# Feature rows of a bidirectional RWKV-7 scan by one transpose per head and chunk, the gate's low-rank job ahead of the second key job, feature loads held back

## Chip, core and metric

One NeuronCore of a Trainium2 chip runs the whole kernel in one launch. The time is the device time of an execution in microseconds, smaller is better; the figure for a kernel is the median of its runs. All data are float32 in HBM. TensorE (PE) takes them as fp32 matmuls, or as fp32r matmuls on operands split into a high and a low part.

## The reference: what is computed

One layer of a diffusion backbone on 128 context tokens and 1024 latent tokens of width 1024, here laid side by side as T = 1152 columns:

```
h = rmsnorm(x, norm1_g) * (1 + sc1) + sh1
r, k, v, wdf, wdb, adf, adb, gd, cb, cc, cx, gates = split(h @ w_in)
# per direction d (forward, backward), per head of 64:
decay = exp(-exp(w_log(tanh(wd) @ w2)));  a = sigmoid(a0 + ad @ a2);  k_d = k * (1 + (a - 1) * k_a)
sa = S @ (-kk);  S = S * decay + sa (x) (kk * a) + v (x) k_d;  y = S @ r      # step by step in t
o_a = (group_norm(y_f + y_b) + bonus) * (sigmoid(gd) @ gate_g2)
o_b = cb * conv3(cc * cx)
x = x + gt1 * ((g_a * (o_a @ w_pa) + g_b * (o_b @ w_pb)) @ w_o)
x = x + gt2 * (conv_ffn(rmsnorm(x, norm2_g) ...) @ w_down)
```

Outputs are both token streams after a final rmsnorm, and the context's final states S of both directions. The scan is computed in chunks of 64 tokens: inside a chunk b (kk * a) and k_d, each scaled by decays, meet the features of kk and r in 64x64 products, and the triangular system of a chunk is solved by repeated products.

## The kernel before

**Dense work.** `build` makes a list `jobs`; a job is one 128-row tile of `w_in` or of another weight. Each weight tile is loaded (`wraw`), split into `whi` and `wlo` on ACT, DVE or POOL, and multiplied with the activations `h` in three thirds (`th`) of 384 columns: 24 matmuls of 128x384 per third, 72 per job, into one of three PSUM banks `psd`. After each third its evacuation runs (`k_evac`, `r_evac`, `gd_evac` and so on). The order of the list is written out by hand at L685 to 692: low-rank jobs WD and AD, then `rkv(0)` (K0, R0, V0), `rkv(1)`, the gate's low-rank job `T_GD`, the 24 fp32 matmuls of `gjobs` (the gate's second weight g2, loaded as in_g2, on the three `gz` of `gd_evac`), then for each of eight m `rkv(m+2)` and branch b, and the two gates.

**Buffers.** `gz` of `gd_evac` (L560) and `kt` of `k_evac` (L614), and two tiles of branch b, share a pool tag `rot` with four buffers. A kt is squared (`ksq`), reduced per head on PE (`kps`), brought to a reciprocal root on ACT (`kr`), and last read by kr<-kt,par,kr on DVE; `gz` is last read by the matmuls psd<-gz,wraw. `st` has four buffers too.

**The scan.** `Scan` runs beside the dense jobs as a set of streams. `drive` steps a stream between two dense matmuls when a condition holds and its time on a model clock (`K.clk`) has come; a priority scheduler then orders each engine's instructions. A pair p is two heads on 128 partitions, and pp is two pairs. `prep_all` (L1022) computes the features of a pair and a third (`prep`) from the low-rank products (`lps` out of `llo`), kk and r, and writes them to DRAM as FA (kk and r) and FB (b and k), one DMA for each per segment, with all 128 partitions. 36 items (4 pp x 9 chunk pairs, 8 blocks e each) go through `prep2_all` (L1040): wait for `ready`, load `E`, `O` (FA by head parity) and `BK` (FB), then `prep2`: the gram matmuls `gpb` and `gpk` (64x64 weights from BK, 64x128), the scaling of BK by the decay on ACT, and the transposition of BK to token rows (`bps`, evacuated to `BT`). bps is 32 fp32 matmuls per item against a 64x64 identity, one for each e, head h and a (b or k), into the half `HS[h if a else 1 - h]` of PSUM. Then `chain` (31 doubling steps on DVE), `merge` (mps), `scan` (px and py, the state `Wt`) and `finish` (fps). A scan step is px<-SX,G, DVE's copy of the state (Wt, L1387), px<-Wt,BT and py<-G,Wt.

**Queues.** Nearly all DMAs are issued by SP, in order; an issue that has to wait for a buffer or for data holds up all behind it. fb<-ak in the profile is the write of FB, BK<-fb, E<-fa and O<-fa the loads of an item, gs<-gz the write of the gate's result.

Of the kernel before, what the change touches and what calls it, by code (L numbers as in the profile page):

```python
# [22 lines left out]
C = 64  # L23
# [9 lines left out]
T_R, T_K, T_V, T_WD, T_AD, T_GD, T_CB, T_CC, T_CX, T_GA, T_GB = 0, 8, 16, 24, 25, 26, 27, 35, 43, 51, 59  # L33
# [308 lines left out]
def build(tc, ins, outs, dbg=None):  # L342
    K = Kern(tc, ins, outs)
# [3 lines left out]
    with es:  # L347
# [162 lines left out]
        with ExitStack() as ea:  # L510
# [130 lines left out]
            def rkv(m):  # L641
                job(T_K + m, k_evac(m))
                job(T_R + m, r_evac(m))
                job(T_V + m, v_evac(m))
# [38 lines left out]
                return ev  # L683

            rkv(0)  # L685
            rkv(1)
            job(T_GD, gd_evac)
            gjobs()
            for m in range(8):
                if m + 2 < 8:  # L690
# [293 lines left out]
class Scan:  # L984
# [4 lines left out]
    def __init__(self, K, const, apool, par, pc, mask, ident, bones, x0, hw0, hka, oka, dr):  # L989
        self.K, self.nc, self.pc, self.dr = K, K.nc, pc, dr  # L990
        self.mask, self.ident, self.bones, self.x0 = mask, ident, bones, x0
        self.hw0, self.hka, self.oka = hw0, hka, oka
        self.eps = const.tile([P, 1], F32, name="gneps", tag="gneps")
        K.nc.gpsimd.memset(self.eps, GN_EPS)
        self.psx = apool("psx", 1, PSUM)
        self.psy = apool("psy", 1, PSUM)
        self.psm = apool("psm", 3, PSUM)
        self.sets = apool("sets", 3)
        self.one = apool("one", 1)
        self.two = apool("two", 2)  # L1000
        self.ys = apool("ys", 4)
        self.fin = apool("fin", 1)
        self.drp = apool("drp", 2, DRAM)
        nc = K.nc
        self.reset = self.one.tile([P, TH], F32, name="reset", tag="reset")
        nc.gpsimd.memset(self.reset, 1.0)
        nc.gpsimd.memset(self.reset.rearrange("p (c t) -> p c t", t=C)[:, :, 0:1], 0.0)
        self.e65 = self.one.tile([P, 6, C + 1], F32, name="e65", tag="e65")
        nc.gpsimd.memset(self.e65[:, :, 0:1], 1.0)
        self.lwl = self.one.tile([P, 4, P], F32R, name="lwlo", tag="lwlo")  # L1010
        nc.gpsimd.memset(self.lwl[64:128].bitcast(F32), 0.0)
        self.items = [(pp, n) for pp in range(4) for n in range(9)]
        self.info = {}

        self.W = self.one.tile([P, 2, 4, 2, C], F32, name="Wt", tag="Wt")
        self.y, self.PC = {}, {}
        self.NY = 4

    def start(self):
        K = self.K  # L1020
        ev = K.events
        N = len(self.items)  # L1022

        def prep_all(s):
            yield lambda: ("kk", 0, 0) in ev and ("r", 0, 0) in ev
            self.lora_in(0, 0)
            for p in range(NPAIR):
                yield lambda: ("kk", p, 0) in ev and ("r", p, 0) in ev
                yield from self.lora_w(s, p)
                for th in (0, 2, 1):  # L1030
                    yield lambda: ("kk", p, th) in ev and ("r", p, th) in ev
                    yield from self.prep(s, p, th)
                    ev.add(("prep", p, th))

        def ready(i, what):
            pp, n = self.items[i]
            ths = {n // 3, (7 - n) // 3} if n < 8 else {2}
            return all((what, 2 * pp + q, th) in ev for q in range(2) for th in ths)

        def prep2_all(s):  # L1040
            for i, (pp, n) in enumerate(self.items):
                yield lambda: ready(i, "prep") and (i < 3 or ("scan", i - 3) in ev)
                self.features(s, i, pp, n)
                s.t = K.clk.now + 2500
                yield
                yield from self.prep2(s, i, pp, n)
                ev.add(("prep2", i))

        def vfill_all(s):
            for i, (pp, n) in enumerate(self.items):  # L1050
                yield lambda: ready(i, "v")
                yield from self.vfill(s, i, pp, n)

        def load_all(s):
            for i in range(N):
                yield lambda: ("gram", i) in ev and (i < 2 or ("chain", i - 2) in ev)
                self.chain_load(i)
                s.t = K.clk.now + 2000
                yield
                ev.add(("load", i))  # L1060

        def chain_all(s):
            for i in range(N):
                yield lambda: ("load", i) in ev
                yield from self.chain(s, i)
                ev.add(("chain", i))

        def merge_all(s):
            for i in range(N):
                yield lambda: ("chain", i) in ev  # L1070
                s.t = K.clk.now + 5000
                yield
                yield from self.merge(s, i)
                ev.add(("merge", i))

        def scan_all(s):
            for i, (pp, n) in enumerate(self.items):
                yield lambda: ("merge", i) in ev and ("prep2", i) in ev
                yield from self.scan(s, i, pp, n)
                ev.add(("scan", i))  # L1080
                if n >= 4:
                    key = 7 - n if n < 8 else 8
                    K.spawn(lambda s2, pp=pp, key=key: self.finish(s2, pp, key), 4, gate=1000, ahead=0)

        K.spawn(scan_all, 0, ahead=0)
        K.spawn(merge_all, 0.5, ahead=0)
        K.spawn(vfill_all, 0.7, ahead=600)
        K.spawn(chain_all, 2, ahead=100)
        K.spawn(load_all, 1.5, ahead=0)
        K.spawn(prep2_all, 1, ahead=-300)  # L1090
        K.spawn(prep_all, 3, gate=1500, ahead=1000)
# [14 lines left out]
    def prep(self, s, p, th):  # L1106
# [15 lines left out]
        for d in range(2):  # L1122
# [52 lines left out]
            for a, b in segs:  # L1175
                g0 = t0 + a if d == 0 or t0 + a >= TL else TL - t0 - b
                K.act(s, PC[:, q, d, g0 // C:(g0 + b - a) // C], e65[:, a // C:b // C, C], AF.Copy)
                for dst, src in (("FA", FAo), ("FB", B)):
                    K.dma(dr[dst][pp][:, q, d, 2 * g0:2 * (g0 + b - a)],
                          src[:, a // C:b // C].rearrange("p c a t -> p (c a t)"), "fa")  # L1180
            yield

    def lora_in(self, th, d):
# [24 lines left out]
    def prep2(self, s, i, pp, n):  # L1208
        K = self.K
        E, O, G, BT, BK = (self.info[i][k] for k in ("E", "O", "G", "BT", "BK"))  # L1210


        HS = [slice(0, 64), slice(64, 128)]
        for q in range(2):
            es = slice(4 * q, 4 * q + 4)
            gb, gk = [self.psm.tile([P, 512], F32, name=nm, tag="psm").rearrange("p (c t) -> p c t", t=2 * C)
                      for nm in ("gpb", "gpk")]
            calls = []
            for e in range(4 * q, 4 * q + 4):
                for ps, a in ((gb, 1), (gk, 0)):  # L1220
                    for h in range(2):
                        o = HS[h if a else 1 - h]
                        calls.append(lambda ps=ps, a=a, h=h, e=e, o=o: K.mm(
                            ps[o, e - 4 * q, :], BK[HS[h], e, a, :], (E, O)[h][HS[h], e, :], True, True, 85))
            K.group(calls)
            s.t = K.clk.now
            mk = lambda sl: self.mask[sl].to_broadcast([sl.stop - sl.start, 4, 2 * C])
            K.tt(s, G[:, es, :], gb, mk(slice(0, P)), ALU.mult)
            for h in range(2):
                o = HS[1 - h]  # L1230
                K.tt(s, (E, O)[h][o, es, :], gk[o], mk(o), ALU.mult)
            yield
        self.to_blocks(s, i)
        K.events.add(("gram", i))
        yield
        yield lambda: i < 2 or ("scan", i - 2) in K.events

        for x in range(4):
            for c in range(2):
                b = BK[:, 2 * x + c].rearrange("p a t -> p (a t)")  # L1240
                K.act(s, b, b, AF.Identity, scale=self.PCc(i, c)[:, x])
        yield
        pv = [self.psm.tile([P, 512], F32, name="bps", tag="psm").rearrange("p (e t) -> p e t", t=C) for _ in range(2)]
        K.group([lambda e=e, a=a, h=h: K.mm(pv[h][HS[h if a else 1 - h], e, :], BK[HS[h], e, a, :],
                                            self.ident[HS[h], HS[h]], True, True, 45)
                 for e in range(8)[::-1] for a in range(2) for h in range(2)])
        s.t = K.clk.now
        for h in range(2):
            K.act(s, BT[:, h], pv[h], AF.Copy)
        yield  # L1250
# [282 lines left out]
```

## Time and profile before

| | |
|---|---|
| median of 3 runs | 3004.88 us (3001.0 to 3005.53) |
| the profiled execution | 2994.76 us, span 2993.0 us |
| granted TensorE clock, mean | 0.972 |
| PE busy | 2771.6 us (93%) |
| DVE busy | 2009.7 us (67%) |
| ACT busy | 1266.4 us (42%) |
| DMA | 388.50 MB, mean 130 GB/s |

Times in the rows are microseconds from the start of the span, of the one profiled execution. In the program's stages: up to about 297 us normalization, the low-rank jobs, K0 to V1 and the gate; to 1082 dense jobs with the first 12 items of the scan; to 1787 the other 24 items beside dense matmuls; then the rest of w_pb, w_pa, w_o and the FFN. A busy PE counts records that overlap, and record ends are modelled. An fp32 matmul leaves two records.

### The profile page before, as it was taken

Reading aid. Unit: us, or ns where it says so; the run is one execution under the profiler, and the core shown is the slowest. Engines: PE = TensorE matmul, PEld = TensorE weight load, DVE = VectorE, ACT = ScalarE, POOL = GpSimd, SP = SyncE. Lnnn points to the kernel's source line nnn. Section 1 sums busy time; section 2 is a strip of 40 time slices with the busy share of each in tenths; the row PEclk is TensorE's granted clock in tenths of the full one; section 3 lists DMA queues with packets and bytes.
Section 4 is the critical chain, followed back from the end, with each engine's and each line's share of the span. In section 5 each row is a group of like instructions: output and inputs, shape, how many; then the busy total and the mean of one; then the engine's idle time right before and its main releaser. Section 6 shows DMA issues by size and latency. Waiting matters only on the chain. (4 is left out here: it accounts for less than half of the span.)

```text
span 2993.0 us, 63336 instructions
## 1 busy us (share of the span) xinstructions
PE 2771.6 (93%) x24762; PEld 2514.2 (84%) x24762; DVE 2009.7 (67%) x5039; ACT 1266.4 (42%) x2540; POOL 318.9 (11%) x342
## 2 busy tenths in 40 slices
PE   7886989999989988988998999899999999999997
PEld 3774778878778877777777789899999999999996
DVE  8367666677568779989877865965555454454556
ACT  5464536454545633334543544023443241424243
POOL 3211111111111111111111112100000000000001
PEclk9997999999999999999999999999999999999999
DMA  4577646464655644544554538853211111111112
GB/s 191 179 240 204 197 121 209 145 180 143 184 172 166 197 118 127 136 115 122 148 136 120 137 101 279 291 165 98 68 43 36 50 40 45 41 41 43 41 44 81
DMA packets 425937, 388.50 MB, mean 130 GB/s; under 512 B 189477, under 2 KB 362405, under 8 KB 425637
## 3 DMA queue, kind: packets, MB, share of 16 engines
q1 hardware_dynamic: 379558, 360.84, 39.6%
q0 software_dynamic: 6912, 18.88, 2.3%
q10 hardware_dynamic: 39168, 4.73, 1.0%
q8 instruction: 195, 3.19, 0.5%
q14 instruction: 104, 0.85, 0.1%
HBM read 268.17 MB, written 116.13 MB: 128 GB/s over the span
## 5 line engine op out<-in xcount | busy, mean ns | idle before, releaser
L89 PE MATMUL psd<-h,whi 128*128 128x384 f32 x3216 | 909.3, 355 | 20.4 <-ACT h L105 9.3
L89 PEld LDWEIGHTS psd<-h,whi 128*128 128x128 f32 x3216 | 592.3, 192 | 58.6 <-issue 12.6
L89 PE MATMUL psd<-h,wlo 128*128 128x384 f32 x1608 | 564.5, 352 | 3.6 <-POOL wlo L110 3.6
L89 PE MATMUL psd<-g,whi 128*128 128x384 f32 (+1 forms) x2112 | 543.2, 338 | 0.0
L105 ACT ACTIVATE whi<-wraw 128x512 fp32r<-128x512 f32 (+2 forms) x334 | 198.4, 595 | 457.5 <-PE psd L89 358.6
L89 PEld LDWEIGHTS psd<-g,whi 128*128 128x128 f32 x2112 | 383.5, 188 | 0.3
L89 PE MATMUL psd<-g,wlo 128*128 128x384 f32 (+1 forms) x1056 | 355.9, 337 | 0.0
L110 POOL TENSOR_TENSOR wlo<-wraw,whi 128x512 fp32r<-128x512 f32 x148 | 207.1, 1402 | 1208.6 <-ACT whi L105 1057.4
L89 PEld LDWEIGHTS psd<-h,wlo 128*128 128x128 f32 x1608 | 309.3, 192 | 17.3 <-POOL wlo L110 5.2
L110 DVE TENSOR_TENSOR X<-X,Xt 128x60 f32<-128x60 f32 (+24 forms) x1116 | 258.0, 233 | 27.3
L110 DVE TENSOR_TENSOR Xt<-X,Dm 128x60 f32<-128x60 f32 (+24 forms) x1116 | 257.4, 233 | 27.0
L89 PE MATMUL psd<-a,whi 128*128 128x384 f32 x864 | 219.0, 334 | 0.0
L89 PE MATMUL psd<-x,whi 128*128 128x384 f32 x768 | 199.7, 341 | 8.0 <-ACT x L105 4.4
L89 PEld LDWEIGHTS psd<-g,wlo 128*128 128x128 f32 x1056 | 199.3, 189 | 0.0
L110 DVE TENSOR_TENSOR wlo<-wraw,whi 128x512 fp32r<-128x512 f32 (+2 forms) x186 | 113.7, 612 | 102.9 <-ACT whi L105 102.9
L89 PEld LDWEIGHTS psd<-a,whi 128*128 128x128 f32 x864 | 156.0, 188 | 0.0
L110 DVE TENSOR_TENSOR fu<-psd,rs 128x384 f32<-128x384 f32 x132 | 73.4, 556 | 117.3 <-PE psd L89 105.2
L89 PEld LDWEIGHTS psd<-x,whi 128*128 128x128 f32 x768 | 140.6, 191 | 10.3 <-ACT x L105 4.7
L89 PE MATMUL psd<-a,wlo 128*128 128x384 f32 x432 | 144.0, 334 | 0.0
L122 DVE SCALAR_TENSOR_TENSOR x<-psd,mod,x 128x384 f32<-128x384 f32 (+3 forms) x160 | 79.2, 515 | 93.9 <-PE psd L89 93.8
L105 ACT ACTIVATE BK<-BK,PC 128x128 f32<-128x128 f32 x288 | 93.2, 392 | 102.2 <-PE gpk L89 77.9
L89 PE MATMUL psd<-x,wlo 128*128 128x384 f32 x384 | 130.5, 340 | 5.4 <-DVE wlo L110 5.4
(206 smaller groups left out, 4917.7 us busy)
## 6 DMA issues: line engine op xcount, KB each, us to landing
wraw<-in_w_in SPq DMA_DIRECT2D x134, 256.0 KB, 3.2
wraw<-in_w_up SPq DMA_DIRECT2D x88, 256.0 KB, 2.6
llo<-lo SPq DMA_DIRECT2D x98, 192.0 KB, 2.7
BK<-fb SPq DMA_DIRECT2D x36, 512.0 KB, 4.8
Dm<-Dd POOLq DMA_DIRECT2D x144, 128.0 KB, 3.6
wx<-in_wmb SPq DMA_DIRECT2D x32, 512.0 KB, 5.3
fa<-fa SPq DMA_DIRECT2D x40, 384.0 KB, 2.7
fb<-ak SPq DMA_DIRECT2D x40, 384.0 KB, 3.0
```

The source lines that it names most:

```text
L89: return self.nc.tensor.matmul(out, lhsT=lhsT, rhs=rhs, start=start, stop=stop)
L105: self.nc.scalar.activation(out, in_, func, bias=bias, scale=scale)
L110: e.tensor_tensor(out, a, b, op)
L122: self.nc.vector.scalar_tensor_tensor(out, a, sc, b, op0, op1)
```

## The change

Four edits. The gate's low-rank job moves between `rkv(0)` and `rkv(1)`, while `gjobs` stays behind `rkv(1)`. `prep_all` notes, in place of an event, a time on the model clock 5000 ns after the features' issue, and the items' loads are ready from then on. FB is written so that on partitions 0 to 63 (the even head) b and k change places, by two DMAs with runs of 64 floats beside one DMA for partitions 64 to 127; the gram matmuls pick b and k accordingly. The 32 bps matmuls of an item become 16 transposes, each of one head's 128 columns (b and k of one e) to 128 partitions.

```diff
--- before.py
+++ after.py
@@ -683,8 +683,8 @@
                 return ev
 
             rkv(0)
+            job(T_GD, gd_evac)
             rkv(1)
-            job(T_GD, gd_evac)
             gjobs()
             for m in range(8):
                 if m + 2 < 8:
@@ -1013,7 +1013,7 @@
         self.info = {}
 
         self.W = self.one.tile([P, 2, 4, 2, C], F32, name="Wt", tag="Wt")
-        self.y, self.PC = {}, {}
+        self.y, self.PC, self.made = {}, {}, {}
         self.NY = 4
 
     def start(self):
@@ -1030,12 +1030,15 @@
                 for th in (0, 2, 1):
                     yield lambda: ("kk", p, th) in ev and ("r", p, th) in ev
                     yield from self.prep(s, p, th)
-                    ev.add(("prep", p, th))
+                    self.made[p, th] = K.clk.now + 5000
 
         def ready(i, what):
             pp, n = self.items[i]
             ths = {n // 3, (7 - n) // 3} if n < 8 else {2}
-            return all((what, 2 * pp + q, th) in ev for q in range(2) for th in ths)
+            keys = [(2 * pp + q, th) for q in range(2) for th in ths]
+            if what == "prep":
+                return all(self.made.get(k, 1e12) <= K.clk.now for k in keys)
+            return all((what, *k) in ev for k in keys)
 
         def prep2_all(s):
             for i, (pp, n) in enumerate(self.items):
@@ -1175,9 +1178,13 @@
             for a, b in segs:
                 g0 = t0 + a if d == 0 or t0 + a >= TL else TL - t0 - b
                 K.act(s, PC[:, q, d, g0 // C:(g0 + b - a) // C], e65[:, a // C:b // C, C], AF.Copy)
-                for dst, src in (("FA", FAo), ("FB", B)):
-                    K.dma(dr[dst][pp][:, q, d, 2 * g0:2 * (g0 + b - a)],
-                          src[:, a // C:b // C].rearrange("p c a t -> p (c a t)"), "fa")
+                cols = slice(2 * g0, 2 * (g0 + b - a))
+                K.dma(dr["FA"][pp][:, q, d, cols], FAo[:, a // C:b // C].rearrange("p c a t -> p (c a t)"), "fa")
+
+                K.dma(dr["FB"][pp][64:128, q, d, cols], B[64:128, a // C:b // C].rearrange("p c a t -> p (c a t)"), "fb")
+                for j in range(2):
+                    K.dma(dr["FB"][pp][0:64, q, d, cols].rearrange("p (c a t) -> p c a t", a=2, t=C)[:, :, j, :],
+                          B[0:64, a // C:b // C, 1 - j, :], "fb")
             yield
 
     def lora_in(self, th, d):
@@ -1221,7 +1228,7 @@
                     for h in range(2):
                         o = HS[h if a else 1 - h]
                         calls.append(lambda ps=ps, a=a, h=h, e=e, o=o: K.mm(
-                            ps[o, e - 4 * q, :], BK[HS[h], e, a, :], (E, O)[h][HS[h], e, :], True, True, 85))
+                            ps[o, e - 4 * q, :], BK[HS[h], e, a if h else 1 - a, :], (E, O)[h][HS[h], e, :], True, True, 85))
             K.group(calls)
             s.t = K.clk.now
             mk = lambda sl: self.mask[sl].to_broadcast([sl.stop - sl.start, 4, 2 * C])
@@ -1241,9 +1248,9 @@
                 K.act(s, b, b, AF.Identity, scale=self.PCc(i, c)[:, x])
         yield
         pv = [self.psm.tile([P, 512], F32, name="bps", tag="psm").rearrange("p (e t) -> p e t", t=C) for _ in range(2)]
-        K.group([lambda e=e, a=a, h=h: K.mm(pv[h][HS[h if a else 1 - h], e, :], BK[HS[h], e, a, :],
-                                            self.ident[HS[h], HS[h]], True, True, 45)
-                 for e in range(8)[::-1] for a in range(2) for h in range(2)])
+        K.group([lambda e=e, h=h: K.transp(pv[h][:, e, :], BK[HS[h], e].rearrange("p a t -> p (a t)"),
+                                           self.ident[HS[h], HS[h]], cost=40)
+                 for e in range(8)[::-1] for h in range(2)])
         s.t = K.clk.now
         for h in range(2):
             K.act(s, BT[:, h], pv[h], AF.Copy)
```

PE around item 14's scan steps, before. mps are the merge's products, psd<-h the dense matmuls, `x16` several of a kind in a row:

```order
L89 MATMUL mps<-G,RSt 32x32
L89 MATMUL bps<-ident,BK 64x64 x3
L89 MATMUL mps<-G,RSt 32x32 x15
L89 MATMUL bps<-ident,BK 64x64 x13
L89 MATMUL px<-SX,G 64x64 x8
L89 MATMUL bps<-ident,BK 64x64 x14
L89 MATMUL px<-Wt,BT 64x64 x8
L89 MATMUL py<-G,Wt 64x64 x8
L89 MATMUL bps<-ident,BK 64x64 x2
L89 MATMUL psd<-h_417,wlo 128x384
L89 MATMUL psd<-h_419,whi 128x384
```

The same place after:

```order
L89 MATMUL mps<-G,RSt 32x32
L100 MATMUL bps<-ident,BK 128x64 x3
L89 MATMUL mps<-G,RSt 32x32 x15
L100 MATMUL bps<-ident,BK 128x64 x12
L89 MATMUL px<-SX,G 64x64 x8
L100 MATMUL bps<-ident,BK 128x64
L89 MATMUL psd<-h_422,whi 128x384
L89 MATMUL psd<-h_421,wlo 128x384
L89 MATMUL psd<-h_423,whi 128x384
L89 MATMUL psd<-h_424,whi 128x384
L89 MATMUL psd<-h_423,wlo 128x384
L89 MATMUL psd<-h_425,whi 128x384
```

The transposes stand almost wholly ahead of px<-SX,G, and six dense matmuls now follow px<-SX,G and one transpose, with px<-Wt,BT behind them; there, 14 bps stood. Over the kernel PE has 1152 bps fewer and 576 transposes more.

ACT in the second key job K1, before (kr<-ksq is the reciprocal root):

```order
L105 ACTIVATE kt<-psd 128x384
L105 ACTIVATE ak<-ak,oka,hka 128x6x64
L105 ACTIVATE ksq<-kt,par 128x384
L105 ACTIVATE ak<-ak 128x6x64
L105 ACTIVATE kt<-psd 128x384
L105 ACT_TABLE_LOAD
L105 ACTIVATE kr_1361<-ksq 128x384
```

The same place after:

```order
L105 ACTIVATE ksq<-kt,par 128x384
L105 ACTIVATE ak<-lps,hw_533 128x6x64
L105 ACTIVATE ak<-ak,oka,hka 128x6x64
L105 ACT_TABLE_LOAD
L105 ACTIVATE kr_1503<-ksq 128x384
L105 ACTIVATE ak<-ak 128x6x64
L105 ACTIVATE whi<-wraw 128x512
L105 ACTIVATE bt<-ak 128x384
L105 ACTIVATE whi<-wraw 128x512
L105 ACT_TABLE_LOAD
L105 ACTIVATE thw<-lps,hw_533 128x384
L105 ACTIVATE kt<-psd 128x384
```

Before, the second kt comes after the first one's square and ahead of its kr<-ksq; now it stands behind the first one's kr<-ksq and pieces of the features' preparation. The evacuations of R1 (sz) follow the third kt.

SP where the first items' features are written and loaded, before:

```order
L128 DMA wraw<-in_g 128x512
L128 DMA E<-fa_114 64x4x256
L128 DMA bs_123<-bt 128x384
L128 DMA krk<-ks_87 128x384
L128 DMA fb_118<-ak 128x512
L128 DMA fb_118<-ak 128x256
L128 DMA krk<-kks_95 128x384
L128 DMA krk<-rs_79 128x384
L128 DMA O<-fa_114 64x4x256
L128 DMA BK<-fb_118 128x4x256
L128 DMA fa_114<-fa 128x768
```

The same place after:

```order
L128 DMA E<-fa_114 64x4x256
L128 DMA O<-fa_114 64x4x256
L128 DMA bs_123<-bt 128x384
L128 DMA fb_118<-ak 64x512
L128 DMA fb_118<-ak 64x4x64 x2
L128 DMA fb_118<-ak 64x256
L128 DMA fb_118<-ak 64x2x64 x2
L128 DMA krk<-ks_87 128x384
L128 DMA krk<-kks_95 128x384
L128 DMA krk<-rs_79 128x384
L128 DMA BK<-fb_118 128x4x256
L128 DMA E<-fa_114 64x4x256
```

The in_g2 load (wraw<-in_g) is gone from here to an earlier place, the first loads of E and O stand in a row, and a segment's fb write is three issues where it was one. SP's DMAs go from 2078 to 2190.

## Rows read from the trace of the kernel before

**Rows 1.** Busy time of each engine by stage, and in the stretch 210 to 300 us. Columns: stretch and its length, busy us (instructions) of PE, PE's weight loads, DVE, ACT and POOL, granted TensorE clock, DMA share, GB/s.

```profile
130.00:297.00 167.00, 123.93 (x854) 102.22 (x852) 110.35 (x267) 100.79 (x220) 21.26 (x23) 0.86 0.73 230
297.00:1082.00 785.00, 719.80 (x6952) 632.75 (x6951) 537.83 (x1358) 395.56 (x854) 120.49 (x116) 0.96 0.57 170
1082.00:1787.00 705.00, 648.47 (x9896) 544.43 (x9891) 594.49 (x2128) 291.88 (x653) 99.98 (x137) 0.99 0.48 126
1787.00:1943.00 156.00, 142.69 (x804) 139.48 (x801) 118.92 (x202) 47.32 (x91) 28.89 (x19) 0.97 0.82 274
1943.00:2993.00 1050.00, 1032.89 (x5878) 1025.27 (x5876) 568.02 (x951) 371.94 (x626) 12.71 (x10) 0.99 0.19 60
...
210.00:300.00 90.00, 54.19 (x454) 37.38 (x454) 64.38 (x207) 42.46 (x101) 8.54 (x14) 0.72 0.71 210
```

**Rows 2.** What PE waited for: tile, line, releaser: us in total, times, longest.

```profile
PE px L89 <- DVE Wt L1387: 14.5, 28, 1.2
PE gpb L89 <- DMA BK<-fb: 14.1, 4, 8.1
...
PE psd L89 <- ACT gz L105: 7.5, 3, 3.5
...
PE psd L89 <- DMA wraw<-in_g: 6.9, 1, 6.9
PE gpb L89 <- DMA gs<-gz: 5.6, 1, 5.6
```

**Rows 3.** Timeline of PE in item 14: start, busy us, instruction, count of records, idle time before it and its releaser.

```profile
1155.92 0.73 PE L89 MATMUL bps<-ident,BK 64*64 64x64 f32 x22
...
1157.36 0.64 PE L89 MATMUL bps<-ident,BK 64*64 64x64 f32 x30
1158.46 0.69 PE L89 MATMUL px<-Wt,BT 128*64 128x64 f32 x16 [0.47 <-DVE Wt L1387]
...
1159.59 0.40 PE L89 MATMUL bps<-ident,BK 64*64 64x64 f32 x8
1159.92 0.44 PE L89 MATMUL psd<-h,whi 128*128 128x384 f32 x1
```

**Rows 4.** The group of bps among PE's groups by shape: count, busy us, mean ns, idle time before.

```profile
L89 PE MATMUL bps<-ident,BK 64*64 64x64 f32 x2304 | 82.1, 230 | 1.1 <-issue 0.8 <-DVE O L110 0.4
```

**Rows 5.** Timeline of PE: two other groups of transposes, at 40.51 and 138.97 us.

```profile
40.51 0.41 PE L100 MATMUL modps<-ident,mrow 2*128 2x2 f32 x4
...
138.97 0.49 PE L100 MATMUL vps<-ident,vz 128*128 128x128 f32 x3
```

**Rows 6.** Timelines of ACT (the three kt of K1) and of DVE (their last readers).

```profile
156.10 0.48 ACT L105 ACTIVATE kt<-psd 128x384 f32<-128x384 f32 x1
...
160.24 0.49 ACT L105 ACTIVATE kt<-psd 128x384 f32<-128x384 f32 x1 [2.15 <-PE psd L89]
...
170.48 0.47 ACT L105 ACTIVATE kt<-psd 128x384 f32<-128x384 f32 x1
...
164.39 0.62 DVE L122 SCALAR_TENSOR_TENSOR kr<-kt,par,kr 128x384 f32<-128x384 f32 x1
...
173.67 0.62 DVE L122 SCALAR_TENSOR_TENSOR kr<-kt,par,kr 128x384 f32<-128x384 f32 x1
...
177.52 0.62 DVE L122 SCALAR_TENSOR_TENSOR kr<-kt,par,kr 128x384 f32<-128x384 f32 x1
```

**Rows 7.** Timeline of PE: the first gate matmuls of g2, the first grams of items 0 and 1, K2's first dense matmul.

```profile
224.19 7.14 PE L89 MATMUL psd<-gz,wraw 128*128 128x384 f32 x14 [6.89 <-DMA wraw<-in_g]
...
233.03 0.29 PE L89 MATMUL gpb<-E,BK 64*64 64x128 f32 x1 [1.70 <-DMA BK<-fb]
...
249.20 0.44 PE L89 MATMUL gpb<-E,BK 64*64 64x128 f32 x1 [8.06 <-DMA BK<-fb]
...
296.83 1.09 PE L89 MATMUL psd<-h,whi 128*128 128x384 f32 x1
```

**Rows 8.** What SP's queue waited for most, and its timeline at the BK loads of items 0 and 1.

```profile
SPq L128 <- DVE wlo L110: 745.6, 179, 10.6
...
227.31 0.54 SPq L128 DMA_DIRECT2D BK<-fb  x1
...
242.02 0.54 SPq L128 DMA_DIRECT2D BK<-fb  x1
```

**Rows 9.** SP's issues of the FB writes and of a load with 256-byte runs (ns min/median/max, first and last start), and DMA issues of the whole kernel (KB each, median us to landing).

```profile
L128 SPq DMA_DIRECT2D fb<-ak x56: 319/338/919, 131.8 to 1051.9; - x56
...
L128 SPq DMA_DIRECT2D Wt<-vt x288: 573/596/1652, 194.2 to 1760.9; - x144
...
fb<-ak SPq DMA_DIRECT2D x40, 384.0 KB, 3.0
...
Xd<-X ACTq DMA_DIRECT2D x144, 32.0 KB, 2.6
```

## The prediction, made before the changed kernel ran

> **What bounds the kernel now.** I read the table of stages first [rows 1]: from 297 us on PE is busy for 92% of every stage (719.80 of 785, 648.47 of 705, 142.69 of 156, 1032.89 of 1050 us), so PE sets the time and only two things move the end: work taken from PE, and time in which PE stands still. In the stretch 130 to 297 us PE works 123.93 of 167 us, and between 210 and 300 us only 54.19 of 90 us, at a granted clock of 0.72: there the end is set by waits. Then the list of what PE waited for [rows 2]; the piece of the timeline around one item's small matmuls [rows 3], an item being one of the 36 chunks of the scan; the cost per shape [rows 4, 5]; and, for the starved stretch, the first gate matmul and the first grams on PE, K1's chain on ACT and DVE, and SP's issues [rows 6 to 9]. DVE is busy 594.49 of 705 us in the scan's own stage [rows 1], so it is the next engine that could pace the items.
>
> **Part 1: 32 small matmuls become 16 transposes per item.** Before, bps is 2304 records (two each for 1152 fp32 matmuls) of 230 ns [rows 4]; four quadrants of the array run side by side, so the records overlap, and what counts is their pace. In [rows 3] the run of 22 takes 0.73 us, less the 0.23 of its last record, or 22.7 ns a record; the run of 30 takes 0.64, or 13.7 ns. Over 2304 records that is 52 us by the first, 32 by the second; starts summed over all items come to the first, and I take 52. After, there are 576 transposes of 128 weight columns and 64 streamed rows. No such row exists. The nearest: four transposes with 128 weight columns and two streamed columns take 0.41 us in all [rows 5], less the 0.20 of a single one about 0.07 apiece; three with 128 streamed columns take 0.49, about 0.11 apiece. Below, if neighbours of different heads overlap as the quadrants do, 0.03. The stream of 64 lies nearer to the first row: 0.06, or 35 us over 576. At 0.03 it is 17, at 0.11 63. In the new order 214 of 500 neighbouring pairs belong to different heads, so a little may overlap; 34. **Minus 18 us** (ends: minus 35, plus 11; with the lower price of before, minus 15 to plus 31).
>
> **Part 2: what stands between the two halves of a scan step.** px<-Wt,BT follows px<-SX,G and needs DVE's copy of the state. Between them PE found only bps in most items, 30 records and 0.41 us in item 14, and then stood still for 0.47 us [rows 3]; the list has 28 such waits, 14.5 us [rows 2]. In the new order the transposes stand ahead, and six dense matmuls fill the gap in nearly all items. K1's groups of 24 matmuls end 4.14 us apart [rows 6], so one is 0.17 us and six are 1.04 us, over the 0.41 + 0.47 that the copy needs. **Minus 13 us**, the rest kept for items whose gap stays short. The ends: 0 if the copy starts later, minus 14.5.
>
> **Part 3: changes of the array's shape.** Before px<-SX,G and a bps both use a 64x64 quarter, and the run at 1157.36 starts with no idle time before it; behind the run of 8 at 1159.59 the dense matmul starts at 1159.92, some 0.16 us after the last bps start [rows 3]. Counted in the orders, boundaries that change the shape next to bps go from 133 to 152: 19 more by 0.1 to 0.16 us, **plus 2 us**. The Trainium skill, page "TensorEngine Tiling (Array Packing)", section Tiling Modes, says that a change of the tiling mode drains TensorE while a change of the tile does not; the 0.16 us agrees, and by that rule with the row's price it is 3 us.
>
> **Part 4: feature writes and hold-back.** One DMA of b and k per segment becomes three: SP has 112 more, 56 of them replacing 56 of 338 ns, 112 with 256-byte runs like Wt<-vt at 596 ns [rows 9]. That is 67 us of SP time between 130 and 1052 us. SP waits 745.6 us for weight buffers alone [rows 8], so after the start this hides; if that cover were gone, SP would be late by at most those 67 us, spread over 900. In the start it does not: BK of items 0 and 1 are issued at 227.31 and 242.02 [rows 8] behind everything else on the queue, and item 0's three DMAs per segment add about 2 us ahead of each. As for landing, Xd<-X, with 128-byte runs, lands in 2.6 us and fb<-ak in 3.0 [rows 9], so I charge none. The Trainium skill, page "DMA: Bandwidth & Descriptors", table at the top, says that transfers under 512 bytes make the DMA engine read, modify and write. No row shows such a price; were the landing to double for it, 3 us would be added at the start and the time be 2992. The hold-back of 5 us is in the scheduler's model clock: it moves the loads of E, O and BK behind other issues in SP's order so that they do not block the queue while the write is still in flight. It costs nothing later, where items wait for dense work and for the scan two items back.
>
> **Part 5: the low-rank gate moved ahead of K1.** The dense work is the same. Gained: the loads of the gate's second weight move up on SP, so the 6.89 us of PE waiting for in_g at 224.19 [rows 7] goes, and perhaps part of the 7.5 for gz and of the 5.6 for gs [rows 2]. Lost: three gz stay in the four-buffer pool until the gate's jobs after V1, and K1's three kt pass through the one buffer left. Each kt is held until kr<-kt on DVE has read it: 156.10 to 165.01, 160.24 to 174.29, 170.48 to 178.14, that is 8.9, 14.0 and 7.7 us, 30.6 in a row [rows 6]. The six groups of K1 and R1 cover 6 x 4.14 = 25 us on PE; R1's evacuations follow the last kt on ACT. I take 3 us of waiting on PE, and pair 1's kk, which item 0's features need, about 8 us later. Item 0's gram was at 233.03 and item 1's at 249.20, after waits of 1.70 and 8.06 for BK [rows 7]; with 8 us of delay, 2 us of extra issues, and the 6.89 us now used by gate matmuls ahead of the gram, K2's dense matmuls start at about 308 instead of 296.83. **Plus 11 us**; the ends are minus 5 (waits go, nothing is late) and plus 36 (worked out below).
>
> **Part 6: the end of the scan.** From 1082 to 1787 us 24 items pass, 29.4 us each [rows 1]. Counted in the orders, 201 more dense matmuls (35 us) stand ahead of item 35's first px and 258 more ahead of the scan's last finishing matmul, as the transposes free PE sooner than DVE's chain frees the items: the scan ends some 15 us later, while the dense list is ahead by as much. Of the 156 us to the next stage little is idle (13 us), and pb's matmuls cover it; **plus 2 us** for x arriving later, 0 to 10.
>
> Sum: -18 - 13 + 2 + 11 + 2 = **-16 us**. The profiled execution took 2994.76 us for a span of 2993.0, which is 10.1 us under the median of the runs, 3004.88. Against it the sum gives 2979; against the median, in which the measurement will be read, **2989**. About 0.2%, 6 us, is what a measurement of this kernel can tell from no change.
>
> **The rivals.**
> *The start is no later.* If the waits for in_g, gz and gs go and kt's chain is hidden, part 5 is -5 instead of +11: -32, or 2973. For it: 36 us of idle in 90 to take from [rows 1]. Against it: the 30.6 us chain and the later pair 1.
> *Nothing is left of it.* If the items are paced by DVE (84% busy in their stage), PE time freed there comes back as idle ahead of pb; parts 1 and 2 then give only some 15 us in all, the start and parts 3 and 6 take 15, and the time is 3005. Against it: dense rows are at hand throughout the stage.
> *The start is much later (slower).* K1's three kt at the slowest row's 14.0 us each make 42 us, 17 more than K1 and R1 cover, and pair 1's preparation moves by 25 us; of those about 19 appear at item 0 and 1, whose grams PE has nothing to put ahead of once the 24 gate matmuls are through. Part 5 is then +36, the sum +9, the time 3014. It decides from a delay of K2's start of about 27 us, where the sum crosses zero. For it: PE waited 14.1 us for BK already [rows 2]. Against it: 14.0 is one row of three.
> *The transposes are slow (slower).* At 0.11 us each part 1 is +11, not -18: +13, or 3018. Against it: the row has twice the streamed columns.
> That the change doesn't do what it says: the orders show 576 transposes in place of 1152 matmuls, so this is not open.
>
> **How the numbers follow.** Forecast 0.50, with its own range 2977 to 2999 (parts 1 and 5 each off by 8); start no later 0.14; nothing left 0.16; start much later 0.13; slow transposes 0.07. The range 2970 to 3015 leaves out the slow transposes and the outer halves of the first and the last case of the start. Faster by over 0.2% (below 2999): 0.48 of the forecast and 0.14, 0.62. Within: 0.16 and 0.02 of the forecast, 0.18. Slower (above 3011): 0.20.
>
> **What the profile after would show.** Part 1: transposes at 0.06 us from start to start, bps beside a pace of 1 us an item. Part 2: px's wait for Wt below 2 us. Part 5: no wait for in_g; K2's first dense matmul between 300 and 315; new waits of psd or kps for kt's release near 170 to 190; item 0's gram near 242. Part 4: fb<-ak in 168 issues, BK landing in about 5 us as before. The prediction is wrong if K2 starts over 20 us later, if the transposes are 0.1 us apart, or if the idle time between 1082 and 1787 grows.

## The result: slower, 3037.89 us

The changed kernel's median is 3037.89 us (4 runs, 3031.9 to 3044.58) beside 3002.94 (4 runs) of the kernel before: a ratio of 1.0118, 95% interval 1.0092 to 1.0143. Faster was forecast, 2989, and the range ended at 3015. The profiled execution took 3035.39 us, its span is 3033.6, 40.6 more than before (the profiled execution of before lies 8 us under that median of 3002.94).

To see where the time went, both traces are cut at the same points of the dense work, by the count of psd matmuls: near the end of the gate's matmuls, 2460 matmuls later, and 2400 further in w_pa. Busy us by stage, after (columns as in [rows 1]):

```profile
130.00:292.30 162.30, 115.35 (x730) 98.20 (x729) 93.71 (x197) 97.44 (x206) 15.73 (x17) 0.82 0.70 207
292.30:1110.20 817.90, 706.41 (x6094) 621.06 (x6093) 531.48 (x1344) 396.70 (x843) 111.88 (x111) 0.91 0.56 161
1110.20:1992.60 882.40, 816.63 (x9990) 702.52 (x9989) 717.61 (x2390) 347.37 (x771) 135.63 (x165) 0.97 0.56 153
1992.60:3033.60 1041.00, 1024.02 (x5827) 1016.42 (x5825) 579.00 (x974) 368.74 (x621) 12.70 (x10) 0.99 0.21 63
```

The same stages before:

```profile
130.00:273.90 143.90, 109.59 (x824) 95.05 (x823) 90.55 (x171) 92.87 (x203) 17.05 (x17) 0.88 0.74 233
273.90:1058.10 784.20, 714.06 (x6632) 623.87 (x6630) 544.53 (x1423) 395.11 (x851) 120.18 (x115) 0.95 0.58 173
1058.10:1951.80 893.70, 820.02 (x11087) 708.76 (x11087) 734.65 (x2375) 349.47 (x769) 133.40 (x161) 0.98 0.54 152
1951.80:2993.00 1041.20, 1024.09 (x5828) 1016.47 (x5826) 559.87 (x936) 370.03 (x622) 12.71 (x10) 0.99 0.19 58
```

The stages take 18.4 us more, 33.7 more, 11.3 less, and 0.2 less. In the second one PE works less than before (706.41 for 714.06 us) and stands still 111.5 us for 70.1; its granted clock falls from 0.95 to 0.91. That is not where the time went: the dense matmuls of this stage alone (psd) are busy for 505.57 us after and 514.79 before. What the stage lost is idle time of PE. It is the stage in which the features of all pairs are written and the first items run beside the dense jobs. What PE waited for over the whole span, after:

```profile
PE gpb L89 <- DMA E<-fa: 32.9, 6, 13.5
PE gpb L89 <- DMA BK<-fb: 17.6, 2, 9.7
...
PE lps L89 <- ACT lwhi L105: 11.8, 3, 8.1
...
PE psd L89 <- ACT gz L105: 11.3, 5, 5.1
PE psd L89 <- ACT whi L105: 11.0, 6, 3.4
...
PE px L89 <- DVE Wt L1394: 8.7, 14, 0.9
```

Against [rows 2], the wait for in_g has gone from the top of the list and that for Wt fell from 14.5 to 8.7 us; grams waiting for BK went from 14.1 to 17.6 us, and those waiting for E, at 7.4 us in the same list of before, now head it with 32.9. The longest wait for E is at 984.59 on PE:

```profile
984.59 0.44 PE L89 MATMUL gpb<-E,BK 64*64 64x128 f32 x1 [13.52 <-DMA E<-fa]
```

SP's queue in the 36 us ahead of it (start, us, issue, count):

```profile
948.30 4.82 SPq L128 DMA_DIRECT2D fb<-ak  x6
...
961.39 2.16 SPq L128 DMA_DIRECT2D fb<-ak  x3
...
965.98 4.55 SPq L128 DMA_DIRECT2D Wt<-vt  x7
...
973.13 1.89 SPq L128 DMA_DIRECT2D fb<-ak  x3
...
978.81 0.57 SPq L128 DMA_DIRECT2D BK<-fb  x1
979.42 0.63 SPq L128 DMA_DIRECT2D E<-fa  x1
```

Twelve FB writes, 8.87 us of issuing, stand ahead of the BK and E that this gram needs, among the loads of the same stretch. From 944 to 981 us SP's own waits add up to 9.2 us; for the rest it issues. What SP pays for the FB writes, and their landing, after, to compare with [rows 9]:

```profile
L128 SPq DMA_DIRECT2D fb<-ak x168: 452/600/1661, 131.5 to 1118.2; - x168
...
fb<-ak SPq DMA_DIRECT2D x40, 192.0 KB, 2.8
fb<-ak SPq DMA_DIRECT2D x80, 96.0 KB, 2.7
```

Summed over the trace, the 168 issues take 101.3 us of SP's time, where the 56 of before took 22.0. They land in 2.8 and 2.7 us, no later than the 3.0 of before.

The start, after: PE waits for a low-rank load that stands in SP's queue, then for item 0's BK; K2's first dense matmul follows at 313.42 (296.83 in [rows 7]).

```profile
225.40 0.66 PE L89 MATMUL lps<-llo,lwhi 128*128 128x384 f32 x1 [6.28 <-DMA llo<-lo]
...
249.33 0.47 PE L89 MATMUL gpb<-E,BK 64*64 64x128 f32 x1 [9.73 <-DMA BK<-fb]
...
313.42 1.02 PE L89 MATMUL psd<-h,whi 128*128 128x384 f32 x1
```

K1's three kt on ACT and their last readers on DVE, after:

```profile
169.61 0.49 ACT L105 ACTIVATE kt<-psd 128x384 f32<-128x384 f32 x1 [1.97 <-PE psd L89]
...
179.86 0.49 ACT L105 ACTIVATE kt<-psd 128x384 f32<-128x384 f32 x1 [0.36 <-DVE kr L122]
...
187.35 0.47 ACT L105 ACTIVATE kt<-psd 128x384 f32<-128x384 f32 x1
...
178.20 1.63 DVE L122 SCALAR_TENSOR_TENSOR kr<-kt,par,kr 128x384 f32<-128x384 f32 x1
...
186.62 0.62 DVE L122 SCALAR_TENSOR_TENSOR kr<-kt,par,kr 128x384 f32<-128x384 f32 x1
...
193.31 0.62 DVE L122 SCALAR_TENSOR_TENSOR kr<-kt,par,kr 128x384 f32<-128x384 f32 x1
```

Each kt now starts when its predecessor was read (178.20 + 1.63 and 179.86; 187.24 and 187.35): the chain of 10.2, 7.4 and 6.6 us is as serial as [rows 6] had let fear. PE's waits from 160 to 215 us come to 5.6 us in all, so R1's matmuls cover most of it.

The group of the transposes, and a slot of item 13 between the halves of a scan step, after:

```profile
L100 PE MATMUL bps<-ident,BK 64*128 64x64 f32 x576 | 48.4, 250 | 0.5 <-ACT BK L105 0.5
...
1207.89 0.68 PE L89 MATMUL px<-SX,G 64*64 64x64 f32 x16
1208.50 0.44 PE L89 MATMUL psd<-h,whi 128*128 128x384 f32 x1
1208.79 0.34 PE L89 MATMUL psd<-h,wlo 128*128 128x384 f32 x1
1208.96 0.51 PE L89 MATMUL psd<-h,whi 128*128 128x384 f32 x2
1209.31 0.33 PE L89 MATMUL psd<-h,wlo 128*128 128x384 f32 x1
1209.48 0.34 PE L89 MATMUL psd<-h,whi 128*128 128x384 f32 x1
1209.75 0.69 PE L89 MATMUL px<-Wt,BT 128*64 128x64 f32 x16
```

Six dense matmuls stand where bps stood in [rows 3], and px<-Wt,BT starts without a wait here.

### The profile page after: what moved, and what is told of

It reads as the page before. It is cut to its first block, busy times and chain, and to the rows that moved or that the text cites. A ratio compares the mean times of both kernels' runs of the same rounds, so it can differ in the third digit from the quotient of the medians.

```text
span 3033.6 us, 60107 instructions
## 1 busy us (share of the span) xinstructions
PE 2766.3 (91%) x23034; PEld 2508.5 (83%) x23034; DVE 2002.4 (66%) x5039; ACT 1269.2 (42%) x2537; POOL 311.8 (10%) x342
## 4 chain that ended last, share of the span: by engine, by line
PE 61%; DVE 21%; DMA 8%; ACT 4%; issue 3%; SPq 3%; ACTq 0%; POOL 0%; DVEq 0%; POOLq 0%
PE psd L89 49%; DVE Xt L110 5%; DVE X L110 4%; PE px L89 3%; SPq L128 3%; PE mps L89 1%; PE gpb L89 1%; DVE ak L110 1%; PE fps L89 1%; PE py L89 1%; PE gpk L89 1%; DVE Mp L110 1%; PE lps L89 1%; DVE G L110 1%; DMA llo<-lo 1%
## 5 line engine op out<-in xcount | busy, mean ns | idle before, releaser
L110 POOL TENSOR_TENSOR wlo<-wraw,whi 128x512 fp32r<-128x512 f32 x148 | 200.4, 1357 | 1129.9 <-ACT whi L105 1003.2
L89 PE MATMUL gpb<-E,BK 64*64 64x128 f32 x576 | 93.5, 308 | 68.6 <-DMA E<-fa 32.9
```

What stands on the lines that cost most here:

```text
L89: return self.nc.tensor.matmul(out, lhsT=lhsT, rhs=rhs, start=start, stop=stop)
L110: e.tensor_tensor(out, a, b, op)
```

## The experiments

Each run is compared with runs of the kernel before on the same chip, so runs on different chips are compared by their differences to it. In t1_transposes and t3_no_writes part of the output is changed, as their texts say: they price the work and are no versions to use. Theories: QUEUE or SPTIME (the FB writes' issues delay what stands behind them on SP), GATE, HOLD (those two edits), the transposes themselves, and TRANSFER or RUNS (the 256-byte runs).

| run | FB issues on SP | us (before) | ratio, 95% interval |
|---|---|---|---|
| t1_transposes | 56 | 2976.06 (3003.60) | 0.9897, 0.9875 to 0.9920 |
| t1_fbwrites | 168 | 3063.48 (3003.60) | 1.0189, 1.0167 to 1.0211 |
| t1_gate | 56 | 2995.77 (3003.60) | 0.9971, 0.9958 to 0.9983 |
| t1_hold | 56 | 2988.65 (3003.60) | 0.9950, 0.9930 to 0.9971 |
| t2_contiguous | 168 | 3052.47 (2996.79) | 1.0181, 1.0161 to 1.0200 |
| t2_pool_queue | 0 | 2963.36 (2996.79) | 0.9878, 0.9854 to 0.9903 |
| t2_gate_hold | 56 | 2966.92 (2996.79) | 0.9901, 0.9878 to 0.9923 |
| t2_mixed | 56 | 2959.18 (2996.79) | 0.9872, 0.9851 to 0.9893 |
| t3_none | 0 | 2994.41 (2997.41) | 0.9994, 0.9977 to 1.0012 |
| t3_two | 112 | 3026.69 (2997.41) | 1.0092, 1.0058 to 1.0125 |
| t3_four | 224 | 3064.13 (2997.41) | 1.0222, 1.0193 to 1.0252 |
| t3_no_writes | 56 | 2946.80 (2997.41) | 0.9824, 0.9788 to 0.9859 |
| t4_layout | 168 | 3000.86 (2996.88) | 1.0017, 1.0001 to 1.0033 |
| t4_no_hold | 168 | 3007.90 (2996.88) | 1.0039, 1.0024 to 1.0054 |
| t4_no_gate | 168 | 3019.50 (2996.88) | 1.0076, 1.0060 to 1.0091 |
| t4_relief | 168 | 2985.43 (2996.88) | 0.9964, 0.9942 to 0.9985 |
| t5_before_relief | 56 | 2990.66 (2996.66) | 0.9986, 0.9970 to 1.0001 |
| t5_mixed_relief | 56 | 2986.35 (2996.66) | 0.9973, 0.9957 to 0.9990 |

### The four edits, one at a time

t1_transposes: the bps hunk of the change alone on the kernel before.

> The kernel before with only the 16 transposes per item; the FB write stays one DMA per segment, so on the even head b and k lie in the other half of BT than the scan takes them from (that part of the output is changed, no work is left out). If the prediction's parts 1 and 2 were right (18 us of PE time and 13 us of waiting), 2970 to 2980. If the transposes themselves cost the loss (0.1 us apart), 3010 to 3020. Theory QUEUE (the extra FB writes on SP are the cause): well below before. Theory GATE or HOLD: the same, they say nothing else on this run.

t1_fbwrites: the FB and gram hunks alone, with bps as 32 matmuls:

```diff
-... K.mm(pv[h][HS[h if a else 1 - h], e, :], BK[HS[h], e, a, :], ...
+... K.mm(pv[h][HS[h if a else 1 - h], e, :], BK[HS[h], e, a if h else 1 - a, :], ...
```

> The kernel before with only the new FB layout: three writes per segment where one was, gram and bps matmuls pick b and k accordingly; still 32 matmuls per item. Theory QUEUE: 168 issues for 56 on SP make features and weights late, 3025 to 3050, with new waits of gpb for E or BK. Theories GATE and HOLD: 3000 to 3008, since SP had slack.

t1_gate: the T_GD hunk alone.

> The kernel before with only the gate's low-rank job ahead of the second key job. Theory GATE (three gz in the four-buffer pool make K1's kt serial and the start late, and all items after it): 3025 or more, K2's dense matmuls from 312 us or later. Theory QUEUE: within 10 us of before, K2 at 295 to 310.

t1_hold: the `made` hunks alone.

> The kernel before with only the loads held back by 5 us of model time. Theory HOLD (the loads of E, O and BK come too late for the grams): 3020 or more, with gpb waiting 20 us or more for E. Theories QUEUE and GATE: within 8 us of before.

The transposes take 27.5 us off, the writes put 59.9 on, the gate takes 7.8 off and the hold-back 15.0. So the loss is in the writes, which cost more than QUEUE's 3025 to 3050. GATE and HOLD fall as causes of their own, and both gain where I had charged 11 us and nothing; for the hold-back's 15 us no theory had room (a miss). With the writes alone the grams wait for E as in the change, 38.6 us for 7.4 before:

```profile
PE gpb L89 <- DMA E<-fa: 38.6, 14, 14.3
```

The four differences add up to +9.6 us, and the change has +35: the rest is in how the edits act together.

### What it is in the writes

t2_contiguous:

```diff
-                for dst, src in (("FA", FAo), ("FB", B)):
...
+                for hs in (slice(64, 128), slice(0, 32), slice(32, 64)):
+                    K.dma(dr["FB"][pp][hs, q, d, cols], B[hs, a // C:b // C].rearrange("p c a t -> p (c a t)"), "fb")
```

> The kernel before, its FB write cut into three contiguous writes per segment (partitions 64 to 127, 0 to 31, 32 to 63), same layout, same bytes, the same 168 issues as the change has, no 256-byte runs. Theory COUNT (what hurts is the number of issues, each with its place in SP's queue): nearly as slow as the run with the new layout, 3035 to 3060. Theory RUNS (what hurts are the runs of 256 bytes, through an issue of 600 ns for 338 or through the transfers themselves): half of the loss or less, 3005 to 3030.

t2_pool_queue:

```diff
-QUEUE = dict(Xw="A", Dm="G")
+QUEUE = dict(Xw="A", Dm="G", fb="G")
```

> The whole change, the three FB writes issued by GpSimd's queue and not by SP's; same writes, same runs. Theory QUEUE (SP's time): the sum of the three other edits, 3003 - 27 - 8 - 15, so 2950 to 2975, and gpb's waits for E and BK back to some 20 us. Theory TRANSFER (the 256-byte runs cost in the DMA engines or land late): 3025 or more, as with the change.

Three contiguous writes cost 55.7 us, as good as all of what the writes with 256-byte runs cost. These two kernels have the same order of instructions on PE, DVE, ACT, GpSimd and SP, so the runs themselves are worth no more than the two ratios can tell apart (1.0181 and 1.0189). On GpSimd's queue the same writes leave the change at 2963.36, 33 us faster than before; its grams wait for BK and E as little as before:

```profile
PE gpb L89 <- DMA BK<-fb: 14.0, 3, 9.7
...
PE gpb L89 <- DMA E<-fa: 9.6, 5, 3.6
```

TRANSFER falls, and QUEUE's forecast came true. But the edit does more than its text says: the key `fb` also names the 40 loads fb<-bs of `finish`, which have left SP too:

```profile
fb<-bs POOLq DMA_DIRECT2D x32, 128.0 KB, 3.2
...
fb<-bs POOLq DMA_DIRECT2D x8, 64.0 KB, 2.3
```

So 208 issues leave SP here and not 168, which leaves it 96 fewer than the kernel before has, and the engines' orders are others than the change's. The same key moves 96 issues in t3_none, not 56. Then the count alone, by t3_two (two contiguous writes), t3_four (four) and t3_none (one write, on GpSimd's queue):

```diff
+                for hs in (slice(64, 128), slice(0, 64)):                                            # t3_two
+                for hs in (slice(64, 96), slice(96, 128), slice(0, 32), slice(32, 64)):              # t3_four
+QUEUE = dict(Xw="A", Dm="G", fb="G")  ...  for hs in (slice(0, 128),):                               # t3_none
```

> The kernel before, its FB write cut into two contiguous writes per segment: 112 issues on SP for 56. Theory SPTIME (each issue ahead of loads and weights costs): about a half of the 56 us that three writes cost, 3020 to 3035. Theory ORDER (any change in the list of instructions gives another schedule, and the schedule with three was a poor one): anywhere between 2985 and 3055, without relation to the count.

> The kernel before, its FB write cut into four contiguous writes per segment: 224 issues for 56. Theory SPTIME: more than with three, 3065 to 3095. Theory ORDER: anywhere between 2985 and 3055.

> The kernel before with its one FB write per segment issued by GpSimd's queue: none of the 56 on SP. Theory SPTIME: 2965 to 2990, if the price of an issue is the same below 56 as above. Theory ORDER: anywhere between 2985 and 3030. If the prediction's slack on SP had been there, 2997 to 3010.

With 0, 56, 112, 168 and 224 issues on SP the differences are -3, 0, +29, +56 and +67 us, so from 56 on the time rises with the count, as SPTIME says; below 56 nothing is gained (a miss: I expected 10 to 30 us, and the 40 loads had left SP as well), and the fourth write adds less than I expected. Summed over the traces, the FB issues take 22.0 us of SP's time before, 63.0 with two writes, 91.4 with three and 105.7 with four: 41, 69 and 84 us more, for 29, 56 and 67 us of device time. In t1_fbwrites it is 99.9, 78 more for 60. In these four kernels 1 us more of FB issuing on SP thus goes with 0.7 to 0.8 us of device time; beside the transposes it is less (t4_layout, below). The issue in t3_four is shorter, 420 ns for the 487 of three:

```profile
L128 SPq DMA_DIRECT2D fb<-ak x224: 302/420/1927, 129.4 to 1128.9; - x112
```

The same row of t2_contiguous:

```profile
L128 SPq DMA_DIRECT2D fb<-ak x168: 412/487/1919, 131.6 to 1104.4; - x168
```

PE is busy for 742 us between 300 and 1110 in the kernel before, 720 with two, 700 with three and 705 with four. The orders of all engines differ between counts, since the scheduler reckons with the issues; how much of the price is SP's own time and how much the order made around it is not told apart by these runs.

t4_relief moves other issues away and leaves the FB writes; t5_before_relief does the same to the kernel before:

```diff
-QUEUE = dict(Xw="A", Dm="G")
+QUEUE = dict(Xw="A", Dm="G", ks="G", kks="G", sp="G")
```

> The whole change, its FB writes still on SP, but 96 other writes (of r, k, kk and v) issued by GpSimd's queue: SP has 2094 DMAs where before had 2078. Theory SPTIME: most of the loss comes back, 2955 to 2990. If it is something in the FB writes themselves (their runs, their place ahead of the same item's loads): 3020 to 3045.

> The kernel before with the same 96 writes (r, k, kk, v) issued by GpSimd's queue. As t3_none showed for the FB writes, SP has room at 2078 DMAs: 2985 to 3005, within 0.5% of before. If it gains 40 us or more, the relief of the change was not about the FB writes.

The change is 35 us above the kernel before and, with the 96 writes moved, 11 us below it, while the same move is worth 6 us to the kernel before, which its interval does not tell from nothing. The 168 FB writes are still on SP, with 104.9 us of issuing. So they do not hurt by what they are, but by coming on top of SP's other issues. Nor is it the start: in t4_relief K2 starts at 316.41, later than the change's 313.42, and what comes back is in the stage behind, 762.1 us for 817.9:

```profile
298.00:1060.10 762.10, 686.08 (x6093) 602.73 (x6092) 535.10 (x1373) 408.28 (x859) 154.49 (x187) 0.96 0.60 174
```

### How the edits act together

t2_gate_hold has both of those edits, t3_no_writes the whole change without the FB writes; t4_layout (transposes and writes), t4_no_hold and t4_no_gate leave one or both out of the change.

> The kernel before with the gate's early place and the held-back loads, without transposes and FB writes. If the two edits add up: 3003 - 8 - 15 = 2980. If they work on the same waits in the start: 2988 to 2996. If they are what makes the change worse than the sum of its parts (which is +10, and +35 was measured): 3005 to 3030.

> The whole change without the new FB writes: transposes, the gate's early place, held-back loads, one FB write per segment (on the even head b and k are in each other's place in BT; nothing is left out). If the parts add up (-27 and -30): 2940 to 2950. If the transposes and the hold-back take the same waits: 2955 to 2970.

> Transposes and the new FB writes, without the gate's early place and the hold-back. If the parts add up: 3000 - 27 + 58 = 3031. If the transposes make the writes dearer: 3040 to 3060. If it is gate and hold-back that lose their 30 us beside the writes: 3025 to 3035, about as slow as the whole change.

> The whole change without the hold-back. If the hold-back is what suffers from a full queue (loads of E and BK issued late, behind the writes): 3005 to 3025, faster than the change. If it still gains its 15 us: 3045 to 3055.

> The whole change with the gate's low-rank job at its old place. If the gate's early place is what suffers (K1's kt serial while SP is late in the start): 3010 to 3030. If it still gains its 8 us: 3040 to 3050.

Without the new writes, gate and hold-back together gain 29.9 us, more than their 7.8 and 15.0; with the transposes it is 50.6. Beside the writes all this turns: layout alone is at +4.0, with the gate +11.0, with the hold-back +22.6, with both +35. So t2_gate_hold is faster than any of its three ranges (from 2980 on), and so is t4_layout (from 3025 on): two misses. t4_no_hold and t4_no_gate lie in the ranges in which the edit left out is the one that suffers. The writes cost 31.5 us on top of the transposes alone (from -27.5 to +4.0), and 86 on top of the other three edits (from -50.6 to +35). Why gate and hold-back change sign beside the writes is not settled. It does not happen in the start: cut at the same points as above, t4_layout is as long as the change up to the gate's matmuls, 162.3 us, and 33.4 us shorter in the stage behind:

```profile
130.00:292.30 162.30, 110.72 (x735) 94.77 (x734) 99.88 (x214) 96.28 (x207) 18.16 (x21) 0.85 0.72 212
292.30:1076.80 784.50, 698.70 (x6075) 611.02 (x6075) 538.42 (x1375) 394.84 (x836) 114.87 (x112) 0.95 0.58 168
```

Its grams wait 14.1 us for E, the change's 32.9, though both have the same FB writes. Each of these kernels has an order of its own, and no run holds it fixed.

### A faster version

t2_mixed needs no new layout: the odd head's b and k lie right for a transpose, the even head keeps its two matmuls. Gate and hold-back as in the change.

```diff
+        K.group([lambda e=e: K.transp(pv[1][:, e, :], BK[HS[1], e].rearrange("p a t -> p (a t)"),
+                                      self.ident[HS[1], HS[1]], cost=40) for e in range(8)[::-1]]
+                + [lambda e=e, a=a: K.mm(pv[0][HS[1 - a], e, :], BK[HS[0], e, a, :], ...
```

> A version without the FB writes: the odd head of each block by a 128-column transpose (b and k lie right for it as they are), the even head by its two 64x64 matmuls as before, with the gate's early place and the held-back loads. 24 instructions per item for 32. If the parts add up: some half of the 27 us of the transposes and 23 us of the other two, 2960 to 2975. If the three edits are in each other's way: 2985 to 3010.

2959.18, 0.9872 of the kernel before, just below what was expected. t2_pool_queue, at 0.9878, can't be told from it. t5_mixed_relief adds the moved queue:

> The version without FB writes (odd heads by transposes, even heads as before, gate early, loads held back) with the 96 writes on GpSimd's queue. If SP is no longer what delays the start: 2950 to 2965, as without it. If the queue still delays weights and loads: 2930 to 2950.

That one was a miss: 2986.35, 27 us slower than without. The same move brought the change 46 us and the kernel before nothing that its interval can tell; why it costs here is not shown.

## Why the prediction was wrong, step by step

**Parts 1 to 3 held as a sum.** It was -29 us, t1_transposes gives -27.5. In the trace of the change neighbouring transposes start 61 ns apart (median of 500 pairs), for the 60 taken; the ends at 30 and 110 ns fell. The wait for Wt went to 8.7 and not below 2, so some 6 of the 13 us came in part 2. With 6 the sum would have been -22: that it came so close is in part luck, and no run shows where the other 5 us lie or prices part 3.

**Part 4 is the step that failed.** It said that 67 us of further issue time hide after the start, as SP waits 745.6 us for weight buffers [rows 8], and put the writes at nothing there. The figure is of the whole span. SP's waits in the kernel before, in the stretch 1943 to 2993 us (first row) and in 130 to 1080 us (the two longest):

```profile
SPq L128 <- DVE wlo L110: 745.1, 177, 10.6
...
SPq L128 <- POOL wlo L110: 80.6, 34, 7.0
SPq L128 <- DVE fa L110: 46.5, 30, 4.7
```

745.1 of the 745.6 us lie in the FFN, where nothing of the scan is left. In the stretch where FB is written the longest entry is 80.6 us. Yet the right stretch alone would not have saved the forecast: all of SP's waits there add up to 498 us of 950, which still looks like room for 67. It is little room, since SP takes its issues in order, and one that waits holds up the loads behind it. In the change SP's waits from 130 to 1080 us are 455 us, so 79 us more of issuing came out of the waits by 44 only. The price was too low as well, 79 us for 67 (101.3 for 22.0). Of the writes' cost I had 2 us in the start in the sum; t1_fbwrites puts it at 60. My own bound of 67 us, if that cover were gone, was near it, but I gave it neither a rival nor a chance. The hold-back, which I costed at nothing, is worth -15 alone. How much of the 60 us is SP's own time and how much the order made around it stays open, and so does why the other edits make it more.

**Part 5 had the places right and the sign wrong.** K1's kt became serial, in_g's wait went, K2 started at 313.42 (forecast about 308, between 300 and 315). That it fits is luck, for most of that lateness is not the gate's. With the gate alone (t1_gate, first row) K2 starts at 300.10 and the kernel gains 7.8 us; with the writes alone (t1_fbwrites, second row) it starts at 309.30:

```profile
300.10 0.81 PE L89 MATMUL psd<-h,whi 128*128 128x384 f32 x2
...
309.30 0.81 PE L89 MATMUL psd<-h,whi 128*128 128x384 f32 x2
```

I had added lateness in the start as if it was PE time lost. Where the 7.8 us are gained no run shows.

**Part 6** gave +2; the stage from item 12 to w_pa is 11.3 us shorter than before, with the transposes' gain in it, so no loss shows there.

**The rivals.** None was it. By their times the nearest were slow transposes (3018), which the 61 ns refute, and a start much later (3014), from K1's chain, which asked for K2 more than 27 us late, where it was 16.6. Of my three signs of being wrong none appeared: K2 was less than 20 us late, the transposes were not 0.1 us apart, and the idle time from 1082 to 1787 us was 56 us before and after. No sign stood for the stretch from 297 to 1082 us, in which most of the loss is. The mechanism, issues ahead of loads on SP, stood in my part 4 as a price and in no rival. The Trainium skill, page "DMA: Bandwidth & Descriptors", section Specifications, says that below 512 bytes a DMA engine reads, modifies and writes. The 256-byte runs of the 96 KB writes land in 2.7 us in t1_fbwrites and the contiguous ones of the same size in 2.6 in t2_contiguous, which is as slow, so no price of that rule shows here.

## What to carry to other kernels

The waits of an in-order queue are not room for what stands behind them: here SP waited for half of the stretch, and 78 us of new issues still cost 60. Such a total is also read in the stretch where the new issues fall, and not over the span. Splitting one DMA into three for a layout adds issues to the queue that has most of them; alone that took twice what the transposes gave alone, and a version with fewer saved matmuls and no new DMA (t2_mixed) beat the change and the kernel before. Edits that gain alone can lose beside one that loads a queue, so each was worth a run with and without it.

## What the runs showed that I had not expected

An issue of a half-partition write costs SP more than a full one: 451 ns at least and 587 at the median for the contiguous 64-partition writes of t3_two, where [rows 9] has 319 and 338 for 128 partitions. Contiguous writes of 32 and 64 partitions together have a median of 487 in t2_contiguous, and with 256-byte runs on two of three it is 598 in t1_fbwrites. Moving the 56 FB writes of the kernel before, and 40 loads, off SP gained nothing (t3_none), though doubling the writes cost 29 us.
